# Two sets of 64 × 64 products per chunk of an RWKV-7 scan, issued together, one product per quadrant of the array

## The chip, the cores and the metric

The kernel runs on one core of one Trainium2 chip. The metric is the device time of one execution in microseconds (us); lower is better. Times of before and after are medians of several executions.

## The reference, cut to what matters

One residual block over 512 positions with 1024 channels. After a norm and one wide projection it has two branches: stick-breaking attention (8 heads of 64) and an RWKV-7 recurrence (8 heads of 64). The branches are gated, projected and added to x; a convolved, gated feed-forward (1024 to 2 × 2816 to 1024) follows. The change lies in the recurrence:

```python
def rwkv7_recurrence(r, w, k, v, a, b):
    # S_t = S_{t-1} diag(w_t) + (S_{t-1} a_t) b_t^T + v_t k_t^T ;  y_t = S_t r_t
    def step(state, inp):
        r_t, w_t, k_t, v_t, a_t, b_t = inp
        sa = jnp.einsum('bhvk,bhk->bhv', state, a_t)
        state = (state * w_t[:, :, None, :] + sa[..., None] * b_t[:, :, None, :]
                 + v_t[..., None] * k_t[:, :, None, :])
        y = jnp.einsum('bhvk,bhk->bhv', state, r_t)
        return state, y
```

The kernel does it by chunks of 64 positions (8 chunks). Inside a chunk, the dependence of each step on the earlier ones is a triangular system; its inverse is called T here. With T, the sum over the chunk's own values (Lak V) and T A, a chunk costs a few matrix products, and only the 64 × 64 state goes from chunk to chunk.

## The kernel before, in words

The program has three phases. Phase 1 (to about 425 us) holds the input projection, both branches and most gates; phase 2 the branch and output projections; phase 3 the feed-forward. Phases 2 and 3 are long rows of full-size matmuls (lines 134 to 136).

In phase 1 three generators share TensorE: `rw_stream` (the recurrence, one call for each of four pairs of heads, p = 0 to 3), `att_stream` (attention, four pairs one after another) and `dense_stream` (the projections, line 868, 24 matmuls to a tile of 128 columns). They are merged by hand in `interleave`: a planner with a clock of its own. Each `yield (cost, lat)` advances that clock by `cost` ns, and says that the stream isn't to be taken up again for `lat` ns more; meanwhile others are taken up, and dense work fills what is left. The dictionary `LAT` holds these waits, one for each step and pair. The order in which instructions are emitted follows from it; the tool chain may still move an instruction whose operands it expects late, but each engine then runs its own queue in order.

Steps of `rw_stream` for one pair that the prediction speaks of (the two heads h of a pair live in the two halves of the 128 partitions; `HROWS` gives for each its own half `hr` and the other, `ho`):

- Lines 560 to 569: products `pa` (32 × 32, line 564), copied by VectorE into U1 (line 568).
- Lines 571 to 580: **Lak V**. For each of 8 chunks and each head one product into the PSUM bank `pl` (line 575): operands in the rows `ho`, output in the partitions `hr`, so head 0 uses the lower left and head 1 the upper right quadrant of the array. ScalarE copies the bank to LV (line 580).
- Lines 582 to 590: products `pu` (32 × 32, line 586) with U1, copied by VectorE into the off-diagonal blocks of TT, which holds T (line 589). They need both copies into U1.
- Lines 592 to 601: **T A**. For each chunk and head one product into the bank `px` (line 595): operands and output in `hr`, so the two quadrants on the diagonal. VectorE scales the bank into XA (line 600), two instructions.
- Lines 609 to 638: the scan over chunks. The first instruction of a chunk is the hop (line 612), 128 × 128 with 64 columns, from TT and LV; from the second chunk on one from XA and the state is added (line 614).

`rbank()` takes the next of three PSUM banks (`psr`), which all steps of `rw_stream` and the norms and transposes of attention share. An f32 product shows as two records in the trace, so 16 products (8 chunks, 2 heads) are 32 records.

Of the kernel before, what the change touches and what calls it, by code (L numbers as in the profile page):

```python
# [8 lines left out]
F32 = mybir.dt.float32  # L9
# [7 lines left out]
P = 128  # L17
# [9 lines left out]
CH = 64  # L27
NC = T // CH
# [24 lines left out]
def hybrid_block(ctx: ExitStack, tc: tile.TileContext, xT, w_in, vecs, decay_up, iclr_up, out_gate_up,  # L53
                 w_branch, w_out, w_up, w_down, out):
    nc = tc.nc
    V, A, G, PE = nc.vector, nc.scalar, nc.gpsimd, nc.tensor
# [21 lines left out]
    def f(ap):  # L78
        return ap.bitcast(F32)
# [62 lines left out]
    def bank(pool=None, tag="pd"):  # L142
        return (pool or psd).tile([P, T], F32, tag=tag, name=tag)
# [41 lines left out]
    TT = cpool.tile([P, NC, P], F32, name="TT")  # L185
# [16 lines left out]
    with tc.tile_pool(name="p0", bufs=1) as p0, \  # L202
# [76 lines left out]
        for j in range(2):  # L279
            hr = slice(64 * j, 64 * j + 64)  # L280
# [4 lines left out]
        for j in range(2):  # L285
            hr, ho = slice(64 * j, 64 * j + 64), slice(64 - 64 * j, 128 - 64 * j)
# [54 lines left out]
    rwp = ph1.enter_context(tc.tile_pool(name="rw", bufs=1, reuse_waits="tile"))  # L341
# [7 lines left out]
    G.tensor_tensor(ogu[1], og_, f(ogu[0]), op=ALU.subtract)  # L349
    og_ = rwp.tile([P, BW], F32, tag="LV", name="og_")  # L350
    for g in range(3):
# [7 lines left out]
    def c3(a):  # L359
        return a.rearrange("p (c t) -> p c t", t=CH)  # L360

    def rbank():
        return bank(psr, "pr")

    HROWS = ((slice(0, 64), slice(64, 128)), (slice(64, 128), slice(0, 64)))
# [38 lines left out]
    def rw_stream(p):  # L404
# [7 lines left out]
        for j, bn in ((0, "db"), (1, "ib")):  # L412
            pl = rbank()
            PE.matmul(pl, lup[j][:, p * P : (p + 1) * P], wl2[j], start=True, stop=False)
            hr = slice(64 * j, 64 * j + 64)
# [54 lines left out]
        for h in range(2):  # L470
            hr = HROWS[h][0]
# [3 lines left out]
        for h in range(2):  # L475
            hr = HROWS[h][0]
# [18 lines left out]
        QAs = []  # L495
        for hf in range(2):
            QA = rwp.tile([P, 4, 2, 256], F32, tag="QA", name="QA", bufs=4)
            QAs.append(QA)
            for c2 in range(2):
                pp = [rbank(), rbank()]  # L500
                for j in range(2):
                    for h, (hr, _) in enumerate(HROWS):
                        ch = 4 * hf + 2 * c2 + j
# [3 lines left out]
                for j in range(2):  # L507
                    for h, (hr, _) in enumerate(HROWS):
                        ch = 4 * hf + 2 * c2 + j
                        PE.matmul(pp[h][:, j * P : (j + 1) * P], BK[hr, ch].rearrange("p s t -> p (s t)"),  # L510
                                  ARV[hr, ch, 0 : 2 + h : 1 + h], start=True, stop=True)
                for h in range(2):
                    V.tensor_tensor(QA[:, 2 * c2 : 2 * c2 + 2, h, 64:192],
                                    pp[h][:, 0:256].rearrange("p (j n) -> p j n", j=2),
                                    maskq[:, None, :].broadcast_to([P, 2, P]), op=ALU.mult)
                for h in range(2):
                    A.copy(QA[:, 2 * c2 : 2 * c2 + 2, h].rearrange("p j (s n) -> p j s n", s=4)[:, :, 0:4:3],
                           pp[h][:, 256:512].rearrange("p (j s n) -> p j s n", j=2, s=2))
                yield (1400, LAT["st1"][p])
            for h, (hr, ho) in enumerate(HROWS):  # L520
                for b in range(2):
                    r0 = 64 * h + 32 * b
                    nc.sync.dma_start(sc[b, h, hf * 4 : hf * 4 + 4].rearrange("q i t -> i q t"),
                                      QA[r0 : r0 + 32, :, h, 128 + 32 * b : 160 + 32 * b])

                vv = QA[ho, :, h, 192:256]
                vs = rwp.tile([P, 4, 1], F32, tag="vs", name="vs", bufs=2)[ho]
# [33 lines left out]
        for ch in range(NC):  # L561
            for h in range(2):
                r0, r1 = slice(64 * h, 64 * h + 32), slice(64 * h + 32, 64 * h + 64)
                PE.matmul(pa[r1, ch * 32 : ch * 32 + 32], QAs[ch // 4][r0, ch % 4, h, 160:192], U1[r0, ch],
                          start=True, stop=True)
        for h in range(2):
            r1 = slice(64 * h + 32, 64 * h + 64)
            V.tensor_copy(U1[r1].rearrange("p q (k g) -> p q g k", g=4),
                          pa[r1, 0:256].rearrange("p (q g k) -> p q g k", q=NC, g=4))
        yield (430, 0)  # L570
        pl = rbank()
        for ch in range(NC):
            for h, (hr, ho) in enumerate(HROWS):
                QA = QAs[ch // 4]
                PE.matmul(pl[hr, ch * CH : (ch + 1) * CH], QA[ho, ch % 4, h, 128:192], QA[ho, ch % 4, h, 192:256],
                          start=True, stop=True)
            if ch == 3:
                yield (530, 0)
        LV = rwp.tile([P, NC, CH], F32, tag="LV", name="LV")
        A.copy(LV, c3(pl))  # L580
        yield (530, LAT["pl"][p])
        pu = rbank()
        for ch in range(NC):
            for h in range(2):
# [4 lines left out]
            V.tensor_copy(TT[r0, :, r1], pu[r0, 0:256].rearrange("p (q n) -> p q n", q=NC))  # L589
        yield (430, LAT["pu"][p])  # L590

        px = rbank()
        for ch in range(NC):
            for h, (hr, _) in enumerate(HROWS):
                PE.matmul(px[hr, ch * CH : (ch + 1) * CH], QAs[ch // 4][hr, ch % 4, h, 192:256], TT[hr, ch, hr],
                          start=True, stop=True)
            if ch == 3:
                yield (530, 0)
        for h, (hr, _) in enumerate(HROWS):
            V.tensor_tensor(XA[hr, :, hr], c3(px)[hr], GC[hr].broadcast_to([64, NC, CH]), op=ALU.mult)  # L600
        yield (530, LAT["x"][p])

        for h, (hr, _) in enumerate(HROWS):
            G.tensor_tensor(RG[hr, 1:NC, h], ARV[hr, 1:NC, 0, :], GC[hr, 1:NC].broadcast_to([64, NC - 1, CH]),
# [4 lines left out]
        for ch in range(NC):  # L609
            QA, ci = QAs[ch // 4], ch % 4  # L610
            pu = rbank()
            PE.matmul(pu[:, 0:CH], TT[:, ch], LV[:, ch], start=True, stop=(ch == 0))
            if ch > 0:
# [4 lines left out]
            if ch < NC - 1:  # L618
                pS = rbank()
                for h in range(2):  # L620
                    PE.matmul(pS[64 * h : 64 * h + 64, 0:64], QA[:, ci, h, 0:64], QA[:, ci, h, 192:256],
                              start=True, stop=True)
# [11 lines left out]
            for h in range(2):  # L634
                PE.matmul(py[64 * h : 64 * h + 64, 0:64], QA[:, ci, h, 192:256], QA[:, ci, h, 64:128],
                          start=(ch == 0), stop=True, skip_group_check=True)
# [3 lines left out]

        rv = rwp.tile([P, T], F32, tag="LV", name="rv")
        yield ("lock", "sl")
# [16 lines left out]
        cs = slice(p * P, (p + 1) * P)  # L659
# [160 lines left out]
    def dense_stream():  # L820
# [27 lines left out]
        while cur:  # L848
# [14 lines left out]
            else:  # L863
# [21 lines left out]
               x=(998, 814, 570, 793))  # L885
# [49 lines left out]
    def chain(*gens):  # L935
        for g in gens:
            yield from g

    interleave([rw_stream(p) for p in range(4)] + [chain(*(att_stream(p) for p in range(4))), dense_stream()])
    ph1.close()  # L940
    state["dma"] = False
# [147 lines left out]
```

## Time and profile before

| | |
|---|---|
| Median of 3 runs | 900.95 us (900.85 to 902.43) |
| The profiled execution's own time | 900.61 us |
| Its span, first to last instruction | 898.9 us |
| Mean granted TensorE clock, share of 2.4 GHz | 0.985 |
| TensorE / VectorE / ScalarE / GpSimd busy | 96% / 62% / 57% / 15% |
| TensorE products of line 575 and of line 595 | 128 records each, 4.8 and 5.4 us busy |

A share of busy time is an average over stages. The busy time of TensorE (PE) merges records that overlap, and the ends of its records are modelled, so that a record can reach past the start of the next. PEld is the load of the stationary operand. In the timeline, records of one kind that follow each other are merged into one row with their count. Idle time ahead of an instruction, and what ended it, stands in square brackets.

### The profile page before, as it was taken

The numbers are of one execution on the slowest core, as the hardware profiler recorded it, in microseconds if no ns is written. First come the engines' busy times: TensorE is split into PE (matmuls) and PEld (weight loads), VectorE is DVE, ScalarE is ACT, GpSimd is POOL, SyncE is SP. The second block draws the span as 40 slices with busy tenths as digits, with TensorE's granted clock in tenths as the row PEclk, the third lists the DMA queues.
The fourth block names the chain that finished last, engine by engine and source line by source line (L and its number), as shares of the span: only waits on it lengthen the run. The fifth ranks groups of instructions, "written<-read, shape, count | busy, mean of one in ns | idle before, by whom it ended". The sixth has DMA issues, their size and how long they took to land.

```text
span 898.9 us, 12743 instructions
## 1 busy us (share of the span) xinstructions
PE 859.5 (96%) x4598; PEld 671.8 (75%) x4598; DVE 561.6 (62%) x1119; ACT 513.3 (57%) x909; POOL 137.8 (15%) x206
## 2 busy tenths in 40 slices
PE   5898889999999989899999999999999999999998
PEld 3576657777777767677788878888888888888886
DVE  7566797796894791345666557777777777522222
ACT  7887879868867773777554445444444444321120
POOL 3342433224333332222000000000000000000000
PEclk9899999999999999999999999999999999999999
DMA  7366646756557527743764433333333333343431
GB/s 212 85 139 127 126 95 135 144 122 132 117 119 160 122 59 162 160 105 81 229 198 124 142 112 94 94 98 102 106 94 93 94 94 94 91 126 100 128 102 41
DMA packets 175135, 106.94 MB, mean 119 GB/s; under 512 B 29568, under 2 KB 156672, under 8 KB 175072
## 3 DMA queue, kind: packets, MB, share of 16 engines
q1 hardware_dynamic: 161392, 81.61, 32.5%
q0 software_dynamic: 10656, 19.40, 13.0%
q10 hardware_dynamic: 3024, 5.11, 1.6%
q8 instruction: 36, 0.59, 0.3%
q14 instruction: 27, 0.22, 0.1%
HBM read 78.31 MB, written 8.39 MB: 96 GB/s over the span
## 4 chain that ended last, share of the span: by engine, by line
PE 52%; DMA 1%; ACT 1%; DVE 0%; issue 0%; ACTq 0%
PE pf L135 17%; PE pf L136 17%; PE pf L134 17%; DMA osb<-ot 1%; PE pd L868 0%; ACT oh L128 0%; ACT L63 0%; PE pd L1023 0%; DVE ol L129 0%; DVE ot L774 0%; DVE x_orw L1045 0%; PE pz L751 0%; ACT w L69 0%; ACT g L69 0%; DVE wtl L757 0%
## 5 line engine op out<-in xcount | busy, mean ns | idle before, releaser
L108 ACT CAST whi<-wraw 128x1024 fp32r<-128x1024 f32 (+1 forms) x132 | 130.0, 985 | 172.0 <-PE pf L135 145.5
L124 DVE TENSOR_TENSOR wlo<-wraw,whi 128x512 fp32r<-128x512 f32 (+1 forms) x178 | 114.3, 679 | 81.9 <-ACT whi L108 81.0
L134 PE MATMUL pf<-h2h,whi 128*128 128x512 f32 x352 | 137.3, 390 | 0.0
L135 PE MATMUL pf<-h2l,whi 128*128 128x512 f32 x352 | 136.9, 389 | 0.0
L136 PE MATMUL pf<-h2h,wlo 128*128 128x512 f32 x352 | 136.9, 389 | 0.0
L868 PE MATMUL pd<-hhi,whi 128*128 128x512 f32 x296 | 122.9, 415 | 0.7 <-ACT whi L108 0.6
L868 PE MATMUL pd<-hlo,whi 128*128 128x512 f32 x296 | 122.4, 414 | 0.0
L122 POOL DMA_DIRECT2D wlo<-wraw x74 | 65.1, 920 | 180.8 <-ACT wlo L121 112.6
L868 PE MATMUL pd<-hhi,wlo 128*128 128x512 f32 x296 | 84.9, 408 | 2.8 <-DMA wlo<-wraw 2.7
L134 PEld LDWEIGHTS pf<-h2h,whi 128*128 128x128 f32 x352 | 66.1, 188 | 14.1 <-issue 0.2
L135 PEld LDWEIGHTS pf<-h2l,whi 128*128 128x128 f32 x352 | 66.1, 188 | 14.0 <-issue 0.2
L136 PEld LDWEIGHTS pf<-h2h,wlo 128*128 128x128 f32 x352 | 66.1, 188 | 13.6
L136 PE MATMUL pf<-dh,wlo 128*128 128x512 f32 x176 | 69.3, 394 | 0.0
L134 PE MATMUL pf<-dh,whi 128*128 128x512 f32 x176 | 69.3, 394 | 0.0
L135 PE MATMUL pf<-dl,whi 128*128 128x512 f32 x176 | 69.3, 394 | 0.0
L868 PEld LDWEIGHTS pd<-hhi,whi 128*128 128x128 f32 x296 | 57.8, 195 | 13.2 <-ACT whi L108 1.1
L868 PEld LDWEIGHTS pd<-hhi,wlo 128*128 128x128 f32 x296 | 53.5, 190 | 17.1 <-DMA wlo<-wraw 6.7
L868 PEld LDWEIGHTS pd<-hlo,whi 128*128 128x128 f32 x296 | 57.5, 194 | 11.5 <-issue 0.7
L1028 DVE TENSOR_TENSOR u<-pf,rs 128x512 f32<-128x512 f32 x44 | 30.3, 688 | 38.7 <-PE pf L136 38.6
L128 ACT CAST dh<-cv 128x512 fp32r<-128x512 f32 x22 | 13.7, 621 | 62.0 <-DVE cv L1037 62.0
L121 ACT ACTIVATE wlo<-whi 128x512 fp32r<-128x512 f32 x74 | 45.4, 628 | 2.7 <-PE pd L868 1.0
L135 PEld LDWEIGHTS pf<-dl,whi 128*128 128x128 f32 x176 | 32.9, 187 | 8.2
(310 smaller groups left out, 1654.9 us busy)
## 6 DMA issues: line engine op xcount, KB each, us to landing
wraw<-in_w_up SPq DMA_DIRECT2D x44, 512.0 KB, 3.7
wraw<-in_w_in SPq DMA_DIRECT2D x41, 512.0 KB, 4.0
wlo<-wraw POOLq DMA_DIRECT2D x74, 256.0 KB, 3.9
wraw<-in_w_down SPq DMA_DIRECT2D x16, 512.0 KB, 4.0
wraw<-in_w_branch SPq DMA_DIRECT2D x16, 256.0 KB, 3.1
wraw<-in_w_out SPq DMA_DIRECT2D x8, 512.0 KB, 4.0
gd<-gs ACTq DMA_DIRECT2D x13, 256.0 KB, 3.2
g<-gd SPq DMA_DIRECT2D x13, 256.0 KB, 2.8
```

The lines of the kernel that those rows point to most:

```text
L108: after(A.copy(hi[:, 0:nk], raw[:, 0:nk]), state["last"])
L121: A.mul(lo[:, 0:n], f(hi[:, k0 : k0 + n]), -1.0)
L122: G.dma_start(lo[:, 0:n], raw[:, k0 : k0 + n], accum_op=ALU.add)
L124: V.tensor_tensor(lo[:, 0:n], raw[:, k0 : k0 + n], f(hi[:, k0 : k0 + n]), op=ALU.subtract)
L128: A.copy(hi, src)
L134: PE.matmul(ps, hi, ah, start=first, stop=False)
L135: PE.matmul(ps, hi, al, start=False, stop=False)
L136: PE.matmul(ps, lo, ah, start=False, stop=last)
L868: PE.matmul(ps, w_, a, start=(n == 0), stop=(n == len(todo) - 1))
L1028: V.tensor_tensor(u, ps, rs2, op=ALU.mult)
```

## The change

The products of Lak V leave their place between the copies into U1 and the products `pu`. They are issued in one loop with the products of T A, after TT is complete: for each chunk four products, in the order `pl` head 0, `px` head 0, `pl` head 1, `px` head 1, that is in four different quadrants, from two banks held together. The copy to LV follows that loop, ahead of XA. The planner is told 650 ns for each half of the loop; before it was told 530 ns for each of four halves. The wait `LAT["pl"]`, unchanged, now follows the products `pa`. No other wait, and no other step, is changed; the hop stays one 128 × 128 product.

```diff
-        yield (430, 0)
-        pl = rbank()
-        for ch in range(NC):
-            for h, (hr, ho) in enumerate(HROWS):
-                QA = QAs[ch // 4]
-                PE.matmul(pl[hr, ch * CH : (ch + 1) * CH], QA[ho, ch % 4, h, 128:192], QA[ho, ch % 4, h, 192:256],
-                          start=True, stop=True)
-            if ch == 3:
-                yield (530, 0)
-        LV = rwp.tile([P, NC, CH], F32, tag="LV", name="LV")
-        A.copy(LV, c3(pl))
-        yield (530, LAT["pl"][p])
+        yield (430, LAT["pl"][p])
         pu = rbank()
...
-        px = rbank()
+
+        pl, px = rbank(), rbank()
         for ch in range(NC):
-            for h, (hr, _) in enumerate(HROWS):
-                PE.matmul(px[hr, ch * CH : (ch + 1) * CH], QAs[ch // 4][hr, ch % 4, h, 192:256], TT[hr, ch, hr],
-                          start=True, stop=True)
+            QA, cs = QAs[ch // 4][:, ch % 4], slice(ch * CH, (ch + 1) * CH)
+            for h, (hr, ho) in enumerate(HROWS):
+                PE.matmul(pl[hr, cs], QA[ho, h, 128:192], QA[ho, h, 192:256], start=True, stop=True)
+                PE.matmul(px[hr, cs], QA[hr, h, 192:256], TT[hr, ch, hr], start=True, stop=True)
             if ch == 3:
-                yield (530, 0)
+                yield (650, 0)
+        LV = rwp.tile([P, NC, CH], F32, tag="LV", name="LV")
+        A.copy(LV, c3(pl))
         for h, (hr, _) in enumerate(HROWS):
             V.tensor_tensor(XA[hr, :, hr], c3(px)[hr], GC[hr].broadcast_to([64, NC, CH]), op=ALU.mult)
-        yield (530, LAT["x"][p])
+        yield (650, LAT["x"][p])
```

## Rows read from the trace of the kernel before

**Rows 1.** Page, part 1: busy time, share of the span, instructions by engine.
```profile
PE 859.5 (96%) x4598; PEld 671.8 (75%) x4598; DVE 561.6 (62%) x1119; ACT 513.3 (57%) x909; POOL 137.8 (15%) x206
```

**Rows 2.** Busy time by stretch; after POOL: granted clock, DMA share, GB/s.
```profile
160.00:200.00 40.00, 39.24 (x245) 29.90 (x244) 33.08 (x99) 29.75 (x60) 10.04 (x11) 1.00 0.63 133
...
240.00:300.00 60.00, 58.12 (x456) 44.54 (x456) 44.44 (x107) 42.64 (x82) 18.79 (x30) 1.00 0.61 125
...
360.00:400.00 40.00, 36.10 (x330) 27.92 (x330) 15.72 (x36) 28.77 (x64) 9.90 (x13) 0.96 0.63 134
...
370.00:380.00 10.00, 7.92 (x82) 5.87 (x82) 5.44 (x9) 9.50 (x18) 3.28 (x4) 0.83 0.78 175
```

**Rows 3.** Groups of TensorE instructions: count, busy us, mean ns, idle before.
```profile
L595 PE MATMUL pr<-TT,QA 64*64 64x64 f32 x128 | 5.4, 225 | 0.0
...
L575 PE MATMUL pr<-QA 64*64 64x64 f32 x128 | 4.8, 222 | 0.5 <-DVE U L568 0.5
```

**Rows 4.** Timeline, pair 0: start us, us, engine, line, operation, count.
```profile
154.82 1.15 PE L575 MATMUL pr<-QA 64*64 64x64 f32 x32
...
155.90 0.69 PE L586 MATMUL pr<-TT,U 32*32 32x32 f32 x32
...
157.88 1.15 PE L595 MATMUL pr<-TT,QA 64*64 64x64 f32 x32
...
160.00 0.33 PE L612 MATMUL pr<-LV,TT 128*128 128x64 f32 x2
```

**Rows 5.** Timeline of TensorE, pairs 1, 2 and 3.
```profile
218.65 1.15 PE L575 MATMUL pr<-QA 64*64 64x64 f32 x32
...
227.26 0.68 PE L595 MATMUL pr<-TT,QA 64*64 64x64 f32 x16
...
229.85 0.33 PE L612 MATMUL pr<-LV,TT 128*128 128x64 f32 x2
...
285.79 0.68 PE L575 MATMUL pr<-QA 64*64 64x64 f32 x16 [0.52 <-DVE U L568]
...
295.12 0.33 PE L595 MATMUL pr<-TT,QA 64*64 64x64 f32 x2
296.12 0.68 PE L595 MATMUL pr<-TT,QA 64*64 64x64 f32 x14
...
297.31 0.68 PE L595 MATMUL pr<-TT,QA 64*64 64x64 f32 x16
...
298.26 0.33 PE L612 MATMUL pr<-LV,TT 128*128 128x64 f32 x2
...
365.43 0.69 PE L564 MATMUL pr<-U,QA 32*32 32x32 f32 x32
366.05 1.15 PE L575 MATMUL pr<-QA 64*64 64x64 f32 x32
...
377.34 1.26 PE L595 MATMUL pr<-TT,QA 64*64 64x64 f32 x32
...
380.01 0.33 PE L612 MATMUL pr<-LV,TT 128*128 128x64 f32 x2
```

**Rows 6.** Timeline: line 510, 64-row products; one head alone, then both heads.
```profile
208.57 0.66 PE L510 MATMUL pr<-ARV,BK 64*128 64x128 f32 x4
...
287.60 0.67 PE L510 MATMUL pr<-ARV,BK 64*128 64x128 f32 x8
```

**Rows 7.** Timeline of ScalarE: the copy to LV in pairs 0 and 3, and a cast ahead.
```profile
156.01 0.59 ACT L580 COPY LV<-pr 128x512 f32<-128x512 f32 x1 [0.18 <-PE pr L575]
...
368.30 1.05 ACT L108 CAST whi<-wraw 128x1024 fp32r<-128x1024 f32 x1 [5.28 <-DMA wraw<-in_w_in]
...
373.05 0.58 ACT L580 COPY LV<-pr 128x512 f32<-128x512 f32 x1
```

**Rows 8.** Timeline, pair 3: the copies into U1, and the products that need them.
```profile
366.17 1.26 DVE L568 COPY U<-pr 32x256 f32<-32x256 f32 x2 [2.41 <-PE pr L564]
...
372.17 0.77 PE L586 MATMUL pr<-TT,U 32*32 32x32 f32 x32 [2.03 <-ACT sq L69]
```

## The prediction

> **What bounds the kernel now.** I read the page's busy times first, then busy time by stretch, then the groups of TensorE, and last the timeline around the changed lines. TensorE is busy 96% of the span, the next engine 62% [rows 1]. By stretch it is busy 39.24 of 40 us and 58.12 of 60 us in the middle of phase 1 at the full clock, but 36.10 of 40 us, with a granted clock of 0.96, where the last pair is handled [rows 2]. So phase 1 is bound by TensorE's own queue, with some slack near its end. The two sets of products are in it four times, once per pair: 128 records each [rows 3]. What the reader should see in the timeline is how long TensorE is kept by them, and who needs their results.
>
> **The products, before.** In pair 0 the 32 records of line 575 begin at 154.82, and the next instruction, line 586, at 155.90: 1.08 us [rows 4]. The row says 1.15; a row's modelled end passes the next start by 0.07, so I take 0.07 off each row. Line 595 costs 1.15 - 0.07 = 1.08 as well [rows 4]. Where the planner put other work into the middle, a half costs 0.68 - 0.07 = 0.61 [rows 5], so two halves 1.22. Pair 1 has line 575 whole and line 595 in halves (one of the two alike rows stands): 2.30. Pair 2 has line 575 in halves, and line 595 in pieces of 2, 14 and 16 records, 0.26 + 0.61 + 0.61: 2.70. Pair 3 has both whole: 1.08 + 1.19 = 2.27 [rows 5]. With pair 0's 2.16 that is 9.4 us of TensorE.
>
> **The products, after.** A last record lasts about 0.22 of the 1.15 [rows 3, 4], so 32 records start within 0.93 us. They belong to two quadrants; 16 steps of two give 58 ns a step. The question is whether four quadrants share a step. For: the products of line 510 use 64 rows and all columns, one head in each half of the rows, and write different banks at the same partitions. Four records of one head alone take 0.66 us, and eight of both heads 0.67 [rows 6]. So halves of the rows that end in the same columns run beside each other, if their banks differ; and that is what `pl` and `px` of one head are to each other. No row shows more than two records abreast. Bounds: two abreast, 64 records take 32 steps, 1.87 + 0.15 of end = 2.0 us whole, and 2.16 in halves; four abreast 16 steps, 1.1 whole and 1.25 in halves. With two pairs whole and two in halves that is 8.4 or 4.7 us against 9.4. I take four abreast, since rows 6 show the harder half of it: **4.7 us less TensorE work**, at the least 1.0.
>
> A rule of the Trainium skill speaks against this (TensorE: Matmul & The Clock Gate, the section on 56 ns against 53.3 ns): starts never come closer than about 25 ns, however few columns a matmul has. By it, 64 records would take an estimated 1.6 us and the end, and the saving would be about 2 us. The 32 × 32 products disagree: 32 records in 0.69 us, less 0.19 for the last, are 16 ns a start [rows 4].
>
> **How much of that reaches the end.** The saved time sits in a stage where TensorE is 97% busy, but others set some of its waits: in pair 3 it stood 2.03 us until ScalarE gave back a bank, and the clock of that 10 us stretch fell to 0.83, 1.7 us more at full clock [rows 2, 8]. Work removed ahead of such a wait lengthens it. Also, the planner now advances 4 × 530 - 2 × 650 = 820 ns less per pair, under waits that it still takes from the same table, so all later work is dealt out differently. I can't work out that order by hand; from nothing lost to all lost is the bound, and I take a third of 4.7 off, 1.5, nearer the small end since rows 2 show TensorE short of idle time nearly everywhere.
>
> **The wait for U1, uncovered.** The products of line 575 stood between the copies into U1 and their first reader, line 586. The two copies end 366.17 + 1.26 = 367.43, 1.4 us after the products `pa` that they wait for [rows 5, 8]. Of the old cover, the 1.1 us of products go; the wait table and dense work remain. In pair 0 only 0.67 us is asked for now (671 in the table), in pair 2 0.61. The cost is at most 0.8 us in each of those two, at least nothing, since dense matmuls are dealt out in blocks of three; I take 0.3 us in all.
>
> **The copy to LV, late.** Before, LV was complete (156.01 + 0.59 = 156.60) 3.4 us ahead of the hop that reads it, at 160.00 [rows 4, 7]. Now it comes after the joint loop, on ScalarE's queue. What stood behind it there (norms, casts of weights) moves up, as far as it was held by it. From the end of `px` to the first hop, the gap was 160.00 - 159.03 = 0.97 us in pair 0, 1.91 in pair 1, 298.26 - 297.99 = 0.27 in pair 2, 1.41 in pair 3 [rows 4, 5]. The copy needs 0.59 + 0.04 of start, if ScalarE is free: it fits in three pairs, and falls 0.4 us short in pair 2, and TensorE, in order, stands there. I take 0.4. XA's two copies on VectorE are where they were, needed one chunk later. No DMA, and nothing of SP's or GpSimd's queues, moves.
>
> **Banks.** Ring order was pa, pl, pu, px; it becomes pa, pu, pl, px, so `pu` takes the next bank, not the one after it. In pair 3 that may spare the 2.03 us [rows 8], or hand it to `pl`; I count nothing, and leave up to 2.0 in the lower end.
>
> **Sum.** -4.7 + 1.5 + 0.3 + 0.4 = -2.5 us on the profiled execution's 900.61 us (span 898.9 and 1.7 around it): 898.1. The median of the runs shown, 900.95, is 0.34 higher: **898.4 us**. A measurement can tell about 0.2%, 1.8 us, from no change, so anything under 899.15 is faster and anything over 902.75 slower.
>
> **Rivals.** (1) *The change doesn't do what it says:* the four don't run abreast. For it: no row with more than two. Against: rows 6. Two abreast save 1.0, less the 0.7 of the two waits: 900.6. The skill's floor of starts, from the rule above, would put it near 899.8 by the estimate there; I give it no chance apart from this case, as rows 4 are against it.
> (2) *Saved and given back:* all four abreast, but the third becomes the whole, as TensorE waits for ScalarE, VectorE or weights at the same instants as before. For it: 36.10 of 40 us busy in the last pair's stretch [rows 2]. Against: the other stretches. 900.95 + 0.7 - 0 to 1: about 901.
> (3) *Slower: LV caught behind a blocked ScalarE.* In pair 3 the products ended at 366.05 + 1.15 = 367.20, and the copy began at 373.05, 5.85 us late, behind a cast that had stood 5.28 us for its weights' DMA [rows 5, 7]; in the other three pairs it began within 0.05. Before, nobody waited; now the first hop would, and with it every matmul queued behind it. Its price in pair 3: 5.85 + 0.59 - 1.41 = 5.0 us, and with the clock's fall beside it (1.7, as in the stretch of rows 2) 6.7. Net of -2.9 without the small wait: 903 to 905. It decides from about 4.7 us of such waits over the four pairs. Against it: the stretch may meet another order, and dense work may be put ahead of the hop.
>
> **How the numbers follow.** The forecast has 0.50; its own range is 894.5 to 899.5, of which 0.02 lies within 0.2% of before. Rival 1 has 0.15 and rival 2 0.11, both within 0.2%; rival 3 has 0.24, slower. Faster 0.48, same 0.28, slower 0.24. The low end takes all of 4.7 and most of the 2.0 of banks: 900.95 - 6.5 = 894.5. The high end goes into rival 3, whose upper half stays out: 903.3. Both signs hold much chance: the likeliest case alone is 894.5 to 899.5.
>
> **What would show it.** In the changed profile the two lines of products should stand in one block of 64 records of about 1.1 us busy, or two of 32 records of 0.6 to 0.7; near 2.1 means two abreast. The idle time ahead of the hop (line 612) on TensorE should name the LV copy in pair 2 at most, under 0.5 us; several us there is rival 3. The idle time ahead of the 32 × 32 products should name the U1 copies for at most 0.8 us. The forecast is wrong if the block is short and the busy time of TensorE falls by 4 us or more while its idle time or its time at the lower clock grows as much.

## The result, and the profile after

The changed kernel takes 906.89 us (median of 6 runs, 904.92 to 909.9), the kernel before 901.66 us (6 runs, 900.79 to 902.72): ratio 1.0075, interval 1.0056 to 1.0094. It is slower, by over 5 us. The forecast was 898.4 us, with 894.5 to 903.3 as its range.

The profiled execution took 905.39 us, span 903.7. Its page, part 1, stands against [rows 1]:

```profile
PE 858.6 (95%) x4598; PEld 671.7 (74%) x4598; DVE 563.4 (62%) x1119; ACT 512.2 (57%) x909; POOL 140.1 (16%) x206
```

The span grew by 4.8 us and TensorE's busy time fell by 0.9: the growth is idle time. Not all of it is the change: the two kernels' TensorE orders agree up to the changed products of pair 0, and there the changed kernel's execution is already 2.2 us late, mostly because an earlier stretch at the lower clock lasted 6.83 us in it and 3.41 in the other. So the timed runs carry the size, and the trace tells where.

**The products themselves.** The joint loop is one block of 64 records in each pair. The rows give its start and end, its length, and the busy time of line 587 (T A) in it, for pairs 1, 2, 3 and 0; line 586 (Lak V) has 32 records in each too:

```profile
229.11:230.27 1.16, 1.16 (x32) 1.02 (x32) 1.00 0.89 261
300.78:301.94 1.16, 1.15 (x32) 1.02 (x32) 1.00 0.04 5
382.63:383.79 1.16, 1.15 (x32) 1.02 (x32) 1.00 1.21 258
157.65:159.86 2.21, 1.15 (x32) 1.04 (x32) 1.00 0.99 253
```

And TensorE's timeline at the start of pair 3's block:

```profile
382.63 0.27 PE L586 MATMUL pr<-QA 64*64 64x64 f32 x1
382.64 0.27 PE L587 MATMUL pr<-TT,QA 64*64 64x64 f32 x1
382.65 0.27 PE L586 MATMUL pr<-QA 64*64 64x64 f32 x1
382.65 0.27 PE L587 MATMUL pr<-TT,QA 64*64 64x64 f32 x1
382.74 0.22 PE L586 MATMUL pr<-QA 64*64 64x64 f32 x1
...
382.80 0.22 PE L586 MATMUL pr<-QA 64*64 64x64 f32 x1
```

Four start within 0.02 us, and from the second four on each four starts some 58 ns after the one before. A whole block of 64 takes 1.16 us, where 32 took 1.15 [rows 4]. In pairs 1 to 3 the change does what it says.

In pair 0 it doesn't. Its block takes 2.21 us, because most of Lak V runs first and most of T A behind it (TensorE, then VectorE):

```profile
157.65 1.14 PE L586 MATMUL pr<-QA 64*64 64x64 f32 x30
158.72 0.94 PE L587 MATMUL pr<-TT,QA 64*64 64x64 f32 x25
```
```profile
157.77 0.85 DVE L578 COPY TT<-pr 32x256 f32<-32x256 f32 x2 [0.49 <-PE pr L575]
```

The copies into TT, which T A needs, end at 157.77 + 0.85 = 158.62, and the products that don't need them stand ahead. To the next start the block keeps TensorE for 2.14 us, where the two sets took 2.16 before. With 1.09 us in each of the other pairs the products take 5.4 us in place of 9.4: they save 4.0 us, and not 4.7.

**Where the time went.** The stretches of [rows 2], in the changed kernel:

```profile
160.00:200.00 40.00, 39.05 (x236) 29.22 (x236) 30.56 (x88) 30.34 (x59) 8.70 (x10) 1.00 0.56 120
240.00:300.00 60.00, 56.23 (x390) 43.33 (x390) 42.10 (x108) 39.84 (x78) 18.00 (x27) 0.97 0.57 119
360.00:400.00 40.00, 33.64 (x304) 25.61 (x304) 13.25 (x30) 25.25 (x54) 9.34 (x12) 0.96 0.72 155
370.00:380.00 10.00, 5.38 (x47) 3.92 (x46) 4.79 (x8) 7.46 (x12) 1.72 (x2) 0.89 0.64 123
```

TensorE is idle for 1.9 us more in 240 to 300 and for 2.5 more in 360 to 400, and the clock, 1.00 before in the former, is 0.97. But the clock fell elsewhere in the execution before: from 140 to 430 us each of the two profiled executions has 10.2 us at 1.2 GHz. So this trace shows the idle time, and the clock's part of the loss shows only in the mean of the runs, below. Before, then changed:

```profile
140.00:430.00 290.00, 278.81 (x2088) 213.87 (x2087) 185.07 (x488) 213.91 (x459) 86.30 (x131) 0.98 0.59 125
```
```profile
140.00:430.00 290.00, 273.96 (x2090) 210.69 (x2090) 187.69 (x490) 213.65 (x460) 89.41 (x132) 0.98 0.57 122
```

What TensorE waited for from 140 to 430 us in the changed kernel (total, times, longest):

```profile
PE pr L575 <- DVE U L568: 3.4, 2, 3.0
PE pr L158 <- DVE sll L639: 2.6, 2, 1.7
PE pd L861 <- DMA wlo<-wraw: 2.1, 3, 1.2
PE pr L505 <- ACT sq L69: 1.8, 1, 1.8
PE pr L605 <- ACT LV L591: 1.4, 2, 1.1
```

The largest is the wait for U1, all of it in pair 3. The same products waited there before too, 2.03 us for a bank [rows 8], so 1.3 us of it are new. Three timelines of that stretch show why, ScalarE's first, then VectorE's, then TensorE's:

```profile
370.71 1.05 ACT L108 CAST whi<-wraw 128x1024 fp32r<-128x1024 f32 x1 [4.73 <-DMA wraw<-in_w_in]
...
374.42 0.63 ACT L69 ACTIVATE sq<-rawk 128x512 f32<-128x512 f32 x1
374.94 0.62 ACT L69 ACTIVATE sq<-sq 128x512 f32<-128x512 f32 x1
```
```profile
375.07 0.69 DVE L671 TENSOR_TENSOR wtl<-sq,wth 128x512 fp32r<-128x512 f32 x1 [8.37 <-ACT sq L69]
375.68 0.75 DVE L677 SCALAR_TENSOR_TENSOR rawq<-rawq,qg,sq 128x512 f32<-128x512 f32 x1
376.46 1.27 DVE L568 COPY U<-pr 32x256 f32<-32x256 f32 x2
```
```profile
368.99 0.69 PE L564 MATMUL pr<-U,QA 32*32 32x32 f32 x32
...
377.12 0.24 PE L575 MATMUL pr<-TT,U 32*32 32x32 f32 x2 [2.96 <-DVE U L568]
```

The products `pa` (line 564) that the copies into U1 need were done at 369.68. But in VectorE's queue the attention norm's two instructions now stand ahead of the copies, and they wait for ScalarE, which stands behind a cast whose weights come late. Before, the copies went first, at 366.17 [rows 8]. It is the order of the queues that differs; the copies themselves cost the same.

### The profile page after: what moved, and what is told of

The parts are those of the page before. It is cut to its first block, busy times and chain, and to the rows that moved or that the text cites. A ratio compares the mean times of both kernels' runs of the same rounds, so it can differ in the third digit from the quotient of the medians.

```text
span 903.7 us, 12719 instructions
## 1 busy us (share of the span) xinstructions
PE 858.6 (95%) x4598; PEld 671.7 (74%) x4598; DVE 563.4 (62%) x1119; ACT 512.2 (57%) x909; POOL 140.1 (16%) x206
## 4 chain that ended last, share of the span: by engine, by line
PE 68%; DVE 11%; ACT 8%; DMA 6%; issue 5%; SPq 1%; POOL 0%; DVEq 0%; ACTq 0%; POOLq 0%
PE pf L136 17%; PE pf L135 16%; PE pf L134 16%; PE pd L861 10%; DMA wraw<-in_w_in 4%; DVE tm L541 2%; DVE U L543 2%; ACT whi L108 2%; SPq L550 1%; PE pr L614 1%; ACT wlo L121 1%; PE pz L744 1%; PE pr L510 1%; DVE ARV L468 1%; PE pr L605 1%
## 5 line engine op out<-in xcount | busy, mean ns | idle before, releaser
L134 PEld LDWEIGHTS pf<-h2h,whi 128*128 128x128 f32 x352 | 66.1, 188 | 14.1 <-issue 0.2
```

The costliest lines, as they stand in the source:

```text
L134: PE.matmul(ps, hi, ah, start=first, stop=False)
```

## The experiments

Two kinds of number are used below: the ratio to the kernel before with its interval, and the *lost clock* of a kernel, which is the span times (1 - mean granted clock), averaged over its timed runs. It is an account of the time at the lower level; what such time costs shows in the dense matmuls, which start 0.43 us apart in the 1.2 GHz stretches and 0.23 us apart in the others (the timeline of `p2_told_sum_kept` below). Idle time at the lower level is in it too, so it is no measured cost. The kernel before loses 12 to 13.5 us so, the changed one 17.7.

**Theories.** A: telling the planner other times deals all later work out differently, and the new order is worse. B: the joint loop itself makes the loss. Two narrower forms of A came up behind the first four kernels. U: the order of VectorE's queue in pair 3, with the copies into U1 behind the norm, makes it. C: TensorE's waits in pair 2 make the clock fall between 280 and 305 us, and that makes it. The first four kernels ran together.

`e1_joint_old_plan`: the changed kernel's instructions, the planner told the old times.

```diff
-        yield (430, LAT["pl"][p])
+        yield (430, 0)
+        yield (530, 0)
+        yield (530, LAT["pl"][p])
...
-                yield (650, 0)
+                yield (530, 0)
...
-        yield (650, LAT["x"][p])
+        yield (530, LAT["x"][p])
```


> The joint loop of the change, but the planner is told what it was told before: 430, 530 and 530 ns with the old wait after the products pa, and 530 + 530 ns for the joint loop, so that all other work is dealt out as before. Theory A (the re-dealt order costs the time: in pair 3 VectorE's queue then holds the copies into U1 behind two steps of attention's norm that wait for ScalarE) expects the order of those copies and of most of the rest as before, no wait of 3 us ahead of the 32 x 32 products in pair 3, and 897 to 900 us where before takes 901 to 902. Theory B (the joint loop itself costs it: LV comes after T A, and the hop, and TensorE's queue with it, waits for ScalarE) expects the loss to stay: 903 to 907 us, with waits at the hop that name LV.

Measured: 896.23 us, ratio 0.995 (0.9932 to 0.9968), faster than both kernels by 5 and by over 10 us. Lost clock 10.3 us. The joint loop takes 5.9 us here (in pairs 0 and 2 part of Lak V again goes ahead), so the products save 3.5.

`e2_plan_alone`: the other half. The two sets of products stay in loops of their own, told the new times.

```diff
+        pl = rbank()
...
+        A.copy(LV, c3(pl))
         yield (430, LAT["pl"][p])
...
-        pl, px = rbank(), rbank()
+        px = rbank()
...
-                PE.matmul(pl[hr, cs], QA[ho, h, 128:192], QA[ho, h, 192:256], start=True, stop=True)
```


> The two sets of products stay where they were, each in a loop of its own, two quadrants at a time; only the planner is told what the change tells it (no time for Lak V, 650 + 650 ns for T A, the wait moved). Theory A expects a slower kernel than the change itself, because the same order is paid for without the 4.7 us of shorter products: 907 to 912 us, with the copies into U1 late in pair 3. Theory B expects no loss: 900 to 903 us.

Measured: 907.16 us, ratio 1.007 (1.0047 to 1.0094). Without a single product issued jointly, the loss is there whole. Together the two say: with the joint loop the old order is 5 us faster, and telling the new times costs more than that. Their waits of TensorE from 140 to 430 us, first those of `e1_joint_old_plan`, then those of `e2_plan_alone`:

```profile
PE pr L607 <- ACT LV L593: 2.1, 2, 1.9
PE pr L564 <- DMA U<-st: 1.7, 3, 0.7
PE pr L589 <- ACT sq L69: 1.7, 1, 1.7
```
```profile
PE pr L158 <- DVE sll L643: 3.1, 2, 2.1
PE pr L505 <- ACT sq L69: 1.8, 1, 1.8
```

In `e1_joint_old_plan` U1 is not waited for at all, though the products that covered its copies are gone there too; the planner is still told their time. In `e2_plan_alone` the wait for U1 is 0.4 us, and the expected late copies of pair 3 are not what it loses by. And the first hop of pair 3 does wait 1.9 us for LV, the mechanism of rival 3 at some two fifths of its price. B falls.

`e3_pair3_alone` and `e4_pairs012`: the change, told times included, in pair 3 only, and in pairs 0 to 2 only (`p < 3`); the other pairs run the code of before.

```diff
+        if p == 3:
+            yield (430, LAT["pl"][p])
...
+        else:
+            yield (430, 0)
+            pl = rbank()
...
```


> The change in pair 3 alone; pairs 0 to 2 as before, so everything up to pair 3 is dealt out as before. Theory A expects the copies into U1 to stand ahead of the second norm step, as before, and a small gain from one pair's products, 899 to 901.5 us. Theory B expects pair 3's wait at the hop for LV, about 1 us in the changed kernel, to take the gain and more: 901.5 to 904 us.

> The change in pairs 0 to 2; pair 3 as before. Theory A expects the order that these three leave behind to bring the late copies into U1 in pair 3 all the same: 904 to 908 us, with 2 to 4 us of TensorE's idle time ahead of pair 3's products. Theory B, which puts the loss into pair 3's own joint loop, expects three pairs' gain of about 3.5 us and no more loss: 898 to 900 us.

Measured: 902.78 us, 1.0027 (1.0011 to 1.0042), and 906.66 us, 1.0064 (1.005 to 1.0078). Pairs 0 to 2 carry the whole loss; pair 3 alone is slower too, where I had expected a gain. The time of `e3_pair3_alone` lies in B's range, but the hop doesn't wait for LV in its trace: the joint loop stands 2.25 us for TT and then runs at 1.2 GHz. In `e4_pairs012` the expected idle time ahead of pair 3's 32 × 32 products is there, 4.1 us, but it names a cast on ScalarE and not U1.

The next four have the joint loop everywhere, as `e1_joint_old_plan`, and part of the new told times; their edits are shown against it. `g1_u1_time_told`: new times in the loop alone.

```diff
-                yield (530, 0)
+                yield (650, 0)
...
-        yield (530, LAT["x"][p])
+        yield (650, LAT["x"][p])
```


> All pairs joint; the planner is told the old 430 + 530 + 530 ns between the products pa and the wait ahead of the 32 x 32 products, and the new 650 + 650 ns for the joint loop. In the built order VectorE's copies into U1 stand behind the norm steps in pair 3, as in the change. Theory U (that order is what costs) expects 902 to 907 us with 2 to 4 us of idle time ahead of pair 3's 32 x 32 products. Theory C (the loss comes from pair 2's stretch, where TensorE's waits make its clock fall) expects 896 to 900 us unless the granted clock falls between 280 and 305 us. A theory that the time told for U1 was all that mattered expects 896 to 898 us.

`g2_loop_time_told`: new times ahead of the 32 × 32 products alone.

```diff
-        yield (430, 0)
-        yield (530, 0)
-        yield (530, LAT["pl"][p])
+        yield (430, LAT["pl"][p])
```


> All pairs joint; the new plan ahead of the 32 x 32 products (nothing told for Lak V), the old 530 + 530 ns for the joint loop. The copies into U1 stand behind the norm steps in pair 3. Theory U expects 902 to 907 us and the idle time ahead of pair 3's 32 x 32 products. Theory C expects 904 to 908 us with a fall of the clock between 280 and 305 us, and without such a fall 897 to 901 us.

`g4_new_plan_pairs01` and `g5_new_plan_pair2`: all new times, in pairs 0 and 1, or in pair 2 alone (`p == 2`).

```diff
+        if p < 2:
+            yield (430, LAT["pl"][p])
+        else:
+            yield (430, 0)
+            yield (530, 0)
+            yield (530, LAT["pl"][p])
...
-                yield (530, 0)
+                yield (650 if p < 2 else 530, 0)
```


> All pairs joint; the planner is told the new times in pairs 0 and 1, the old ones in pairs 2 and 3. In the built order the copies into U1 stand ahead of the second norm step in pair 3, as in the kernel before. Theory U expects 896 to 900 us. Theory C expects 903 to 907 us if pair 2's stretch (280 to 305 us) shows TensorE's waits of 2 to 3 us and a fallen clock, which the new order of pairs 0 and 1 would bring about, and 896 to 900 us if it doesn't.

> All pairs joint; the planner is told the new times in pair 2 alone. The copies into U1 stand ahead of the second norm step in pair 3. Theory U expects 896 to 900 us. Theory C expects 896 to 900 us where TensorE's waits in 280 to 305 us stay under 2 us, and 902 to 906 us where they don't and the clock falls there.

Measured, against 900.04 us: 904.55 (1.0052, 1.0036 to 1.0068), 905.09 (1.0055, 1.0038 to 1.0071), 906.48 (1.0085, 1.0063 to 1.0107), 908.51 (1.0096, 1.0079 to 1.0113). Each part costs about as much as the whole. In `g4_new_plan_pairs01` and `g5_new_plan_pair2` the U1 copies of pair 3 go ahead of the norm and TensorE waits for them 0.4 us at most, and both are slow: U falls as the cause, and is one wait among several that take each other's place. C's fall is in the traces of all four, in `g5_new_plan_pair2` from 280.6 us for 10.2 us.

The last batch asked what it is in the new order. `g6_new_plan_pair3`: as `g4_new_plan_pairs01`, in pair 3 alone (`p == 3`).

> The joint loop in all pairs, the new told times in pair 3 only, the old ones in pairs 0 to 2. If the loss sits in the stretches of pairs 0 to 2 being dealt out anew (clock falls near 218 to 226 and 280 to 305 us), these falls do not come, and the time is e1's plus what pair 3 did alone in e3_pair3_alone (some 2 us over before, less its own saved 1.2): 897 to 900.5. If any order dealt out anew costs the same 8 us or more, wherever it begins, 904.5 to 908.5.

`p1_told_500`: the kernel before, no work changed, 30 ns less told.

```diff
-                yield (530, 0)
+                yield (500, 0)
...
-        yield (530, LAT["pl"][p])
+        yield (500, LAT["pl"][p])
```


> No work is changed: the kernel before, in which the planner is told 500 ns where it was told 530 for the four halves of the two products (120 ns less per pair, against 820 less in the changed kernel). If the table of waits fits the one order for which it holds, and any other order costs clock and waits, 903.5 to 908, ratio above 1.002. If only the large shift of 820 ns hurts, the order stays nearly the same and the time is that of before, 900 to 902.5.

`p2_told_sum_kept`: the changed kernel, the joint loop told as long as both loops were.

```diff
-                yield (650, 0)
+                yield (1060, 0)
...
-        yield (650, LAT["x"][p])
+        yield (1060, LAT["x"][p])
```


> The changed kernel, in which the planner is told 1060 ns for each half of the joint loop in place of 650, so that a pair's told time is in sum what it was before (4 x 530), but the 32x32 products and the U1 copies are dealt out as in the changed kernel. If the shift of all later work by 820 ns a pair makes the loss, most of it goes: 896 to 900. If every order dealt out anew loses, 904 to 908.5, with falls of the clock between 215 and 305 us again.

`g3_lv_on_vector`: `e1_joint_old_plan` with one copy moved to another engine.

```diff
-        A.copy(LV, c3(pl))
+        V.tensor_copy(LV, c3(pl))
```


> The joint loop under the old told times (as e1_joint_old_plan), and the copy of pl to LV on VectorE in place of ScalarE, all four pairs. What is left of rival 3 in e1 is a wait of 1.88 us ahead of pair 3's first hop, which names the LV copy. If that wait is on the path, it goes: 894 to 896 us, ratio about 0.993, no idle time over 0.5 us ahead of the hop that names LV. If it was hidden (the next wait takes it over) or VectorE's queue is as late there, 896 to 899, and the idle time names VectorE.

Measured, against 902.03 us: `g6_new_plan_pair3` 899.98 (0.9975, 0.996 to 0.9991), `p1_told_500` 905.55 (1.0031, 1.0014 to 1.0049), `p2_told_sum_kept` 906.34 (1.0044, 1.0021 to 1.0066), `g3_lv_on_vector` 903.07 (1.0002, 0.9983 to 1.0021). C falls too as the whole cause: the trace of `g6_new_plan_pair3`, faster than before, has its fall (6.83 us from 281.4 us), and that of `p1_told_500`, slower, has none there. `p1_told_500` is the plainest: 30 ns less told in four places of each pair, the same work, and 3.5 us more. It is not the 820 ns by which all later work moved, since `p2_told_sum_kept` gives them back and stays slow. And it need not be the planner: in `g3_lv_on_vector` the wait for LV is gone as meant, and the whole gain of `e1_joint_old_plan` with it: instructions around it changed places on TensorE and ScalarE too, two waits for banks that ScalarE gives back grew, and its lost clock is 15.4 us. Its waits of TensorE, 140 to 430 us (1.6 and 1.7 in `e1_joint_old_plan`):

```profile
PE pr L505 <- ACT sq L69: 4.2, 1, 4.2
PE pr L589 <- ACT sq L69: 3.0, 1, 3.0
```

`p2_told_sum_kept` shows the other part of the loss. Its ScalarE, then its TensorE, in pair 2:

```profile
282.96 1.05 ACT L108 CAST whi<-wraw 128x1024 fp32r<-128x1024 f32 x1 [4.44 <-DMA wraw<-in_w_in]
...
286.60 0.67 ACT L69 ACTIVATE sq<-pr,eps_n 128x512 f32<-128x512 f32 x1
```
```profile
282.36 0.39 PE L861 MATMUL pd<-hhi,whi 128*128 128x512 f32 x1
282.59 0.39 PE L861 MATMUL pd<-hlo,whi 128*128 128x512 f32 x1
...
287.33 0.28 PE L505 MATMUL pr<-ident,BK 64*128 64x64 f32 x2 [3.62 <-ACT sq L69]
...
289.30 0.63 PE L861 MATMUL pd<-hlo,whi 128*128 128x512 f32 x1
289.73 0.63 PE L861 MATMUL pd<-hhi,whi 128*128 128x512 f32 x1
```

Again a cast waits for its weights, the norm behind it holds a bank, and TensorE stands 3.62 us; right behind that, from 287.6 us, it runs at 1.2 GHz for 13.65 us. Busy time by stretch, first of `p2_told_sum_kept`, then of `e1_joint_old_plan` (granted clock behind POOL):

```profile
215.00:310.00 95.00, 89.33 (x716) 68.10 (x716) 64.75 (x164) 62.60 (x133) 32.15 (x50) 0.89 0.58 123
310.00:430.00 120.00, 114.37 (x779) 87.80 (x777) 61.76 (x170) 84.77 (x197) 36.66 (x46) 0.96 0.53 116
```
```profile
215.00:310.00 95.00, 90.60 (x796) 70.44 (x796) 67.55 (x186) 71.31 (x159) 34.45 (x55) 1.00 0.63 133
310.00:430.00 120.00, 113.06 (x750) 87.39 (x749) 60.59 (x152) 82.33 (x178) 32.54 (x41) 0.99 0.54 122
```

Over the timed runs, mean time, lost clock and what is left without it, in us:

| kernel | mean | lost clock | rest |
|---|---|---|---|
| before (with `e1` to `e4`) | 901.2 | 12.2 | 889.0 |
| before (with `g1`, `g2`, `g4`, `g5`) | 899.8 | 11.9 | 887.9 |
| before (with `g3`, `g6`, `p1`, `p2`) | 902.1 | 13.3 | 888.8 |
| changed | 907.2 | 17.7 | 889.5 |
| `e1_joint_old_plan` | 896.7 | 10.3 | 886.4 |
| `e2_plan_alone` | 907.6 | 16.3 | 891.3 |
| `g4_new_plan_pairs01` | 907.4 | 18.6 | 888.8 |
| `g5_new_plan_pair2` | 908.4 | 18.7 | 889.7 |
| `g3_lv_on_vector` | 902.2 | 15.4 | 886.8 |
| `g6_new_plan_pair3` | 900.0 | 15.0 | 885.0 |
| `p1_told_500` | 905.0 | 17.1 | 887.9 |
| `p2_told_sum_kept` | 906.0 | 19.8 | 886.2 |

The changed kernel against `e1_joint_old_plan` is 10.5 us: by this account 7.4 of clock and 3.1 of the rest. Against the kernel before it is 6.0 us, 5.5 of them clock. `p2_told_sum_kept` has the rest of `e1_joint_old_plan`; by the account its loss against that kernel is clock alone, and among its 12 runs the time rises by 0.82 us for each us of lost clock.

Do the waits bring the falls of the clock? Two more kernels were to tell, by making ScalarE hold one bank longer in the kernel before. `d1_bank_held_19` repeats the logarithm three times, `d2_bank_held_37` six times (`range(7)`):

```diff
-            act(sq, pn, AF.Ln, scale=1.0 / 64.0, bias=eps_n)
+            for _ in range(4 if (p, which) == (2, "q") else 1): act(sq, pn, AF.Ln, scale=1.0 / 64.0, bias=eps_n)
```


> The kernel before, products and told times as they were; in pair 2 alone ScalarE runs the logarithm of q's norm three times more over the same bank (the same values again), so that it gives the bank back some 1.9 us later (three times 0.62). TensorE waited there 1.03 us for that bank. Up to that place the order of the work is the one of before; behind it neighbours change places in pair 2. Theory W, a wait of TensorE brings a fall of the clock behind it: a wait of about 2.9 us, the granted clock under 1.00 between 280 and 310 us, where the kernel before has 1.00, the lost clock of the runs up by 1.7 to 6.8 us, and 904 to 910 us. Theory N, the wait costs itself alone: the clock stays at 1.00 there, and 902 to 904.

> As d1_bank_held_19, with six more logarithms in place of three, some 3.7 us. Theory W: a wait of up to 4.7 us, a fall of the clock between 280 and 310 us at least as long as in d1, 907 to 913 us. Theory N: the clock stays at 1.00 there, and 903.5 to 906.

Measured, against 901.84 us: 903.66 (1.0027, 1.0001 to 1.0053) and 903.8 (1.0021, 1.0005 to 1.0038), lost clock 14.8 and 14.1 against 13.5. By the numbers that is theory N, but the condition was not set up: the wait for the bank did not grow but went. The stretch in `d1_bank_held_19`:

```profile
278.00:310.00 32.00, 31.75 (x317) 23.61 (x315) 18.35 (x40) 25.36 (x58) 10.20 (x17) 1.00 0.59 125
```

TensorE is idle there for 0.25 us: the longer instruction made the order change around it, and other work stood in the gap. In `d2_bank_held_37` the order put a wait elsewhere: TensorE stood 2.91 us from 357.3 us on, and the clock fell at 360.11 us, where the kernel before waits 1.15 us at most and its clock stays up. The kept traces of all sixteen kernels go the same way in pair 2. A fall begins between 280 and 293 us in ten of them; ahead of it TensorE had stood for 1.3 to 4.2 us at once in nine, and for 0.8 in one. In the six without it the longest wait there was 1.58 us once (`e1_joint_old_plan`), and 1.03 us or less otherwise. But each of these is another order, so it stays open whether waits bring the falls. The changed kernel's fall at 220.83 us speaks against waits alone: in the 7 us ahead of it TensorE was idle 0.2 us once, but more than half of its instructions there were products of 64 or 32 rows. And in `d2_bank_held_37`, whose order up to pair 2 is that of before, the clock fell at 220.16 us, which it did not in the profiled execution of before. How far the order decides shows at this place: the six kernels with the new told times ahead of the 32 × 32 products in pairs 0 and 1 (the changed one, `e2`, `e4`, `g2`, `g4`, `p2`) all have a fall between 218.9 and 220.8 us in their traces, and of the other ten kernels two have one nearby (220.2 and 218.3 us). So an order makes falls more or less frequent; what in it does so isn't shown.

## Why the prediction was wrong

**Right in three pairs: the products.** In pairs 1 to 3 they run four abreast, 1.16 us a block, 1.1 forecast, and rival 1 is out. In pair 0 they don't, since their order is another, and the term of -4.7 measures -4.0 in the changed kernel. The Trainium skill's floor for starts, about 25 ns (TensorE: Matmul & The Clock Gate, the section on 56 ns against 53.3 ns) does not hold for these: 64 starts lie within 1.16 - 0.22 = 0.94 us, 15 ns each; the measurement decides. In the old order the gain reaches the end: 901.28 - 896.23 = 5.1 us; in the means it is 4.5, of which 1.9 is less lost clock and 2.6 the rest. That this lies close to the -2.5 of the sum is luck: the products save 3.5 us there, and the 1.5 taken off stood for a new order that this kernel doesn't have.

**Wrong: "How much of that reaches the end".** This step failed. It saw that 820 ns less told per pair would deal all later work out differently, said that this order could not be worked out by hand, and then bounded its effect by "from nothing lost to all lost" of the 4.7 us, with 1.5 taken. The bound is false, because it treats the new order as a way to waste the gain, and not as a cost of its own. `e2_plan_alone`, with nothing to waste, measures that cost: 907.16 - 901.28 = 5.9 us. The changed kernel against `e1_joint_old_plan` gives 907.2 - 896.7 = 10.5 for the same step, where the sum had 1.5. The first part of it, waits, I had in mind; the larger, by the account 7.4 us of clock, had no term in the sum (rival 3 alone counted 1.7 for it), though [rows 2] showed the clock at 0.83 and 0.96 where TensorE's work is broken up.

**The wait for U1** was put at 0.3 us, in pairs 0 and 2, by the cover that went. It was 3.4 us in pair 3 (2.96 and 0.41), where the cover had nothing to do with it: `e1_joint_old_plan` lacks the cover and does not wait, while `p1_told_500`, which has the cover, waits 3.5 us there. I looked at what stood ahead of the copies in TensorE's order and not at what could be put ahead of them in VectorE's.

**The copy to LV**: 0.4 us forecast, in pair 2; 1.4 measured, 1.1 of it in pair 3 and the rest in pair 1, none in pair 2. **Banks**: pair 3's wait of 2.03 us [rows 8] went into the one for U1 ahead of the same products, and the one of line 505 for ScalarE's bank came out at 1.8 us, where it was 1.0 before; so nothing gained, as counted.

**The rivals.** Rival 1's second time, near 899.8, is 899.65 by its own terms (900.95 - 2 + 0.7); nothing hangs on it. Rival 2 has the idle time about right: the saved time, 4.0 us, reappears as idle time, 5.5 more over the span where TensorE's records show 29.6 us before and 35.0 now. Its time is not, since in the mean of the runs the clock came on top. Rival 3 has the sign, and the place of one wait, but not the cause: the hop's wait for LV in pair 3 was 1.07 us and not 5.0. The sentence on what would make the forecast wrong is what happened: a short block, and from 140 to 430 us TensorE's busy time fell from 278.8 to 274.0 us with the end no earlier.

## What to carry to other kernels

Where an order is dealt out from times told to a planner, and waits from a table that fits one order, a told time is part of the kernel: change the work and the told time in separate steps. Here the work alone gives 896.23 us (0.995), and that version, `e1_joint_old_plan`, beats both kernels; with honest new times it loses. And before pricing such a change, re-deal the order with no work changed, as `p1_told_500` does: what that costs, 3.5 us there and 5.9 in `e2_plan_alone`, is what any saving of a few us stands against. And look in the trace whether the instructions meant to run together do so in every place: here the tool chain took them apart in one pair of four.

## What the runs showed of the hardware

Four 64 × 64 products on the four quadrants of the array run together at 58 ns a step, as fast as two: 64 records in 1.16 us in pairs 1 to 3 of the changed kernel, 32 in 1.15 us before. At the lower clock a dense matmul starts every 0.43 us, against 0.23. The profiled executions have one to four stretches at 1.2 GHz between 200 and 430 us, of 3.41 to 13.65 us each, and which of them come differs even between executions whose order agrees up to there (before and `d2_bank_held_37`, at 220.16 us), so that the mean over runs, and not one profile, tells how much clock an order loses.
